# A third buffer for raw weights in a hybrid decoder block, paid with one tile of another pool

## The chip, the cores and the metric

The kernel runs on one core of a Trainium2 chip. The metric is device time in microseconds. The kernel before takes 958.78 us, the median of three runs (956.76, 958.78, 961.67). The profile shown below comes from one further execution that took 956.58 us, of which 954.4 us lie between its first and its last instruction.

## The reference, cut to what matters

One layer for 512 tokens of width 1024, all in 32-bit floats:

```
proj = rms_norm(x) @ w_in                      # 1024 x 3096 columns
o_nsa  = nsa_attention(...)                    # 8 heads, 2 KV heads: compressed, selected, window
o_rwkv = rwkv7_time_mix(...)                   # 8 heads, a scan over 512 tokens
x = x + concat(o_nsa, o_rwkv) @ w_out          # 1024 x 1024
x = x + cross_attention(rms_norm(x), rms_norm(mem))   # w_q, w_kv, w_o; 256 memory tokens
h = rms_norm(x)
x = x + (silu(h @ w_gate) * (h @ w_up)) @ w_down      # hidden width 2816
out = rms_norm(x)
```

## The kernel before, in words

**Products in halves.** Each weight and each activation is split into two fp32r parts, a high one and a low one, and a product is three matmuls: high by high, high by low, low by high. So every weight tile passes through three steps before TensorE can use it. A DMA on SP's queue brings 512 KB of raw weights into a tile `w` of the tag `W` (`wload`, line 373). ScalarE casts it into `wh` (tag `WH`, line 339). VectorE subtracts to get `wl` (tag `WL`, line 340). After the subtraction the raw tile is free and the next load into it may start. There are two buffers of each of the three tags.

**The order of the dense products** is the string `ORDER` and the list `items` behind it: the input projection (`L`, `C`, `r`, `m`, `K`, `q`, `v`), the keys and values of the memory (`X0` to `X7`, then `V00` to `V03` and `V10` to `V13`), the output projection of the mixers (`o00` to `o07` for the first 256 tokens, `o10` to `o17` for the rest), then the query and output projections of the cross attention, and the FFN. The generator `bulk` (line 399) walks through this list. Before the products of item n it emits the split of item n+1 and the load of item n+2:

```
            if ld:
                halves(n + 1)
                yield from load(n + 2)
                yield from run(W[n])
                n += 1
```

An item of `w_out` or of the value part of `w_kv_x` is 12 matmuls of 512 columns, an item of the input projection or the FFN 24.

**Who goes first.** `bulk` is one of several generators. Others are `start` (first norm), `rwkv_pair`, `inverse` and `chain` (the RWKV scan, 8 chunks in a row), `attention` with its 16 units (four head pairs by four query blocks), `mem_load`, `norm` and `xatt`. A small planner (`Threads.run`) chooses which generator emits next, by a number (0 for the chain, 2 for the attention, 3 for `bulk`, 4 for the memory norm) and by a clock that adds up matmul costs. The tile framework then orders each engine's instructions, sets every semaphore and gives every tile a slot.

**Tile accounting.** A generator that needs tiles yields a request such as `dict(Q=1)` and goes on only when the planner's count allows it; `th.free(Q=...)` gives back. The planner's count of `Q` starts at `NQ - 7`, as seven of the `NQ` tiles are in use from the start. A tile of tag `Q` is 4 KB per partition, and so is one of tag `W`. The lines that matter here:

```
    tQ = mk("Q", NQ)
    tW = mk("W", 2)
...
        th.free(Q=16, U=4, A=1)          # end of chain(): AR, AM and BKt of four head pairs
...
            th.free(Q=2 if jp < 3 else 6)   # unit(): after the scores of a head pair's last block
...
            yield dict(Q=1)
            oT[jp] = qpair("oT")         # unit(): output of a head pair, read out of PSUM tile pv
            split(*oT[jp], pv)
            th.done(f"o{jp}", 1.5)
```

A unit makes its scores and then waits for the event `o{jp - 1}`, since the PSUM tile `pv` is one for all head pairs. At most three units are open at a time (`KU = 3`).

Of the kernel before, what the change touches and what calls it, by code (L numbers as in the profile page):

```python
# [18 lines left out]
KD = D // 128  # L19
RW0 = 1304  # L20
CW = -0.5 * math.exp(-0.5)
NQ, NT, NU = 29, 10, 4
C_ID, C_TRI, C_BONE, C_CEN, C_MASK, C_VAL = 0, 128, 256, 384, 512, 640


# [39 lines left out]
class Threads:  # L65
# [28 lines left out]
    def run(self):  # L94
        while self.q:
            for t in self.q:
                if isinstance(t[3], str) and t[3] in self.ev:
                    t[2], t[3] = max(t[2], self.ev[t[3]]) + ADJ.get(t[5].split()[0] + ":%d" % t[6], 0.0) + ADJ.get(t[5] + "/%d" % t[6], 0.0), None
            live = [t for t in self.q if self.fits(t)]
            assert live, (self.pools, [(t[5], t[6], t[3]) for t in self.q])  # L100
            ready = [t for t in live if t[2] <= self.clock]
            if not ready:
                self.clock = min(t[2] for t in live)
                continue
            t = min(ready, key=lambda t: (t[0], t[1]))
            if self.dense(t) < DENS:
                t = max(ready, key=lambda t: (t[5] == "bulk", -t[0], -t[1]))
            if t[3]:
                for p, n in t[3].items():
                    if p in self.pools:  # L110
                        self.pools[p] -= n
                t[3] = None
            self.mark(t[5] + ":%d" % t[6])
            t[6] += 1
            self.cur = t[5]
            try:
                with self.ahead(PR.get(t[5].split()[0], 0)):
                    y = next(t[4])
            except StopIteration:
                self.q.remove(t)  # L120
                continue
            if isinstance(y, (str, dict)):
                t[3] = y
            else:
                t[2] = self.clock + y * MUL.get(t[5].split()[0], 1.0) + ADJ.get(t[5].split()[0] + ":%d" % t[6], 0.0) + ADJ.get(t[5] + "/%d" % t[6], 0.0)


def _body(ctx, tc, I, out, dbg=None, upto=99, mark=lambda s: None):
# [10 lines left out]
    def nm(s):  # L139
        cnt[0] += 1  # L140
        return f"{s}_{cnt[0]}"

    def mk(tag, bufs, pool=None):
        def f(shape=(128, 512), dt=F32, n=tag):
            return (pool or pp).tile(list(shape), dt, tag=tag, bufs=bufs, name=nm(n))
        return f
# [8 lines left out]
    tT = mk("T", NT)  # L155
    tU = mk("U", NU)
    tI = mk("WI", 1)
    tW = mk("W", 2)
    tH = mk("WH", 2, hp)
    tL = mk("WL", 2, hp)  # L160
    t5 = mk("s512", 6)
# [237 lines left out]
    def bulk(items, first):  # L399
        todo = [i for i in items if i[0]]  # L400
        raw, W = {}, {}

        def load(n):
            if n < len(todo):
                if len(todo[n]) > 2:
                    yield todo[n][2]
                raw[n] = todo[n][0]()

        def halves(n):
            if n < len(todo):  # L410
                W[n] = raw[n]()

        W[0] = first
        yield "xn0"
        yield from load(1)
        n = 0
        for ld, run, *_ in items:
            if ld:
                halves(n + 1)
                yield from load(n + 2)  # L420
                yield from run(W[n])
                n += 1
            else:
                yield from run(None)
# [1181 lines left out]
    W0.extend([(ALLP, 0, wcols("w_in", RW0 + c, 128))] for c in (1536, 1664))  # L1606
    th.add(0, "start", ordered(start()))
    th.add(3, "bulk", bulk(items, W0))
    th.add(2, "att", attention())
    th.run()  # L1610
# [28 lines left out]
```

## Time and profile before

| | us |
|---|---|
| median of three runs | 958.78 |
| the profiled execution | 956.58 |
| its span, first to last instruction | 954.4 |
| TensorE busy in the span | 908.5 |
| VectorE busy | 508.5 |
| ScalarE busy | 400.9 |
| GpSimd busy | 80.8 |

All positions below are microseconds from the start of the span. The stages on this scale: first norm and RWKV inputs to about 185, attention and scan to about 378, memory values and output projection to about 468, cross attention to about 592, FFN to the end. Matmuls overlap in the trace, so a mean duration of one is longer than the distance from one to the next; for a rate, the busy time of a stretch is divided by its count. A number in square brackets behind a row of the timeline is the engine's idle time just before it, with what ended it.

### The profile page before, as it was taken

The page shows a single profiled execution, that of the slowest core. Times are in us where ns is not written, and L with a number is a line of the kernel's source. Part 1 is how long each engine was busy: PE and PEld are TensorE (multiplying, and loading weights), DVE is VectorE, ACT ScalarE, POOL GpSimd, SP SyncE. Part 2 cuts the span into 40 slices and gives each one's busy share as a digit, 9 for nine tenths or more (in the row PEclk, how much of TensorE's full clock was granted, in tenths as well). Part 3 has the DMA queues.
Part 4 walks back from the last instruction along what each step waited for, and adds up shares of the span by engine and source line. Part 5 has one row for each costly group of instructions (what it writes and reads, how often), then busy time and mean ns, then how long its engine had stood idle before and what let it go on. Part 6 is the DMA issues. An engine that isn't in the chain of part 4 may idle for free.

```text
span 954.4 us, 14532 instructions
## 1 busy us (share of the span) xinstructions
PE 908.5 (95%) x5797; PEld 741.3 (78%) x5797; DVE 508.5 (53%) x991; ACT 400.9 (42%) x738; POOL 80.8 (8%) x128
## 2 busy tenths in 40 slices
PE   6999999999999988879899999999999999999997
PEld 4778777777778766757788888888888888888885
DVE  5366676788565776355555555443343443422235
ACT  4355444347567886334444433332323323212121
POOL 5121110000240010010200002000000000000002
PEclk9999999999999999999999999999999999999998
DMA  7222445736203121774431141323333333242332
GB/s 228 58 66 69 124 113 140 180 89 135 89 3 100 35 56 47 203 214 140 126 89 48 64 142 36 111 89 92 108 89 109 89 90 109 89 129 91 92 107 88
DMA packets 125405, 97.19 MB, mean 102 GB/s; under 512 B 23531, under 2 KB 109873, under 8 KB 125339
## 3 DMA queue, kind: packets, MB, share of 16 engines
q1 hardware_dynamic: 122714, 91.80, 33.8%
q10 hardware_dynamic: 2624, 4.48, 1.8%
q8 instruction: 45, 0.74, 0.4%
q14 instruction: 22, 0.17, 0.1%
HBM read 90.22 MB, written 4.48 MB: 99 GB/s over the span
## 4 chain that ended last, share of the span: by engine, by line
PE 80%; ACT 6%; DVE 6%; DMA 5%; issue 2%; POOL 2%; SPq 0%; ACTq 0%; POOLq 0%; DVEq 0%
PE pj L207 41%; PE acc L207 16%; PE pv L207 3%; DMA w<-in_w_out_dram 2%; ACT wh L339 2%; PE pt L211 2%; PE kx L207 2%; PE sc L207 2%; PE ps L207 2%; PE vg L207 1%; PE ch L207 1%; DVE wl L340 1%; DMA w<-in_w_kv_x_dram 1%; PE tr L211 1%; PE xs L207 1%
## 5 line engine op out<-in xcount | busy, mean ns | idle before, releaser
L207 PE MATMUL pj<-xn,wh 128*128 128x512 f32 (+1 forms) x1280 | 293.3, 378 | 0.8 <-DVE xn L340 0.5
L340 DVE TENSOR_TENSOR wl<-w,wh 128x1024 fp32r<-128x1024 f32 (+1 forms) x130 | 158.5, 1219 | 198.5 <-ACT wh L339 113.8
L207 PEld LDWEIGHTS pj<-xn,wh 128*128 128x128 f32 x1280 | 227.4, 190 | 46.3 <-issue 2.7
L339 ACT CAST wh<-w 128x1024 fp32r<-128x1024 f32 (+1 forms) x131 | 137.0, 1046 | 277.9 <-PE pj L207 144.8
L207 PE MATMUL pj<-xn,wl 128*128 128x512 f32 (+1 forms) x640 | 154.9, 379 | 0.0
L207 PEld LDWEIGHTS pj<-xn,wl 128*128 128x128 f32 x640 | 113.8, 188 | 21.8 <-issue 1.6
L207 PE MATMUL acc<-wh,hid 128*128 128x512 f32 x288 | 68.2, 389 | 0.0
L207 PEld LDWEIGHTS acc<-wh,hid 128*128 128x128 f32 x288 | 54.1, 188 | 11.2
L1474 DVE SCALAR_TENSOR_TENSOR th<-th,pj 128x512 f32<-128x512 f32 x22 | 15.1, 688 | 75.7 <-PE pj L207 75.7
L207 PE MATMUL acc<-wh,oT 128*128 128x512 f32 x128 | 34.6, 413 | 9.4 <-ACT wh L339 6.6
L207 PEld LDWEIGHTS acc<-wh,oT 128*128 128x128 f32 x128 | 24.2, 197 | 16.9 <-ACT wh L339 8.7
L1105 ACT ACTIVATE S<-S,mx 128x128 f32<-128x128 f32 (+3 forms) x64 | 35.3, 552 | 4.3 <-DVE mx L1103 4.2
L207 PE MATMUL acc<-wl,hid 128*128 128x512 f32 x144 | 35.6, 389 | 0.0
L1535 POOL TENSOR_TENSOR xr<-xr,gain 128x512 f32<-128x512 f32 x4 | 5.2, 1288 | 345.3 <-DVE ss L1532 345.3
L1103 DVE CUSTOM_DVE_ANT_0 S<-ps,Bt 128x128 f32<-128x128 f32 (+3 forms) x64 | 29.7, 483 | 8.5 <-PE ps L207 8.3
L207 PE MATMUL ps<-K,q 128*128 128x512 f32 (+2 forms) x96 | 29.7, 390 | 3.4 <-DVE mx L1103 2.3
L207 PEld LDWEIGHTS acc<-wl,hid 128*128 128x128 f32 x144 | 27.0, 188 | 5.6
L207 PE MATMUL pv<-S,Vt 128*64 128x128 f32 x320 | 30.4, 284 | 0.3 <-ACT S L1146 0.2
L211 PE MATMUL pt<-ident,S 128*128 128x128 f32 x160 | 25.8, 280 | 4.2 <-ACT S L1146 4.2
L339 ACT CAST hid<-th 128x512 fp32r<-128x512 f32 x22 | 13.7, 621 | 31.7 <-DVE th L1474 31.7
L211 PEld LDWEIGHTS pt<-ident,S 128*128 128x128 f32 x160 | 18.1, 140 | 9.4 <-ACT S L1146 5.3
L280 POOL TENSOR_TENSOR ss<-ss,kst 128x1 f32<-128x1 f32 x14 | 7.7, 551 | 208.1 <-DVE ss L279 207.1
(298 smaller groups left out, 1302.5 us busy)
## 6 DMA issues: line engine op xcount, KB each, us to landing
w<-in_w_gate_dram SPq DMA_DIRECT2D x22, 512.0 KB, 3.9
w<-in_w_up_dram SPq DMA_DIRECT2D x22, 512.0 KB
w<-in_w_down_dram SPq DMA_DIRECT2D x22, 512.0 KB, 3.5
w<-in_w_in_dram SPq DMA_DIRECT2D x18, 512.0 KB, 5.2
w<-in_w_kv_x_dram SPq DMA_DIRECT2D x16, 512.0 KB, 4.0
w<-in_w_out_dram SPq DMA_DIRECT2D x16, 256.0 KB, 5.1
w<-in_w_out_dram SPq DMA_DIRECT2D x8, 512.0 KB, 3.7
w<-in_w_q_x_dram SPq DMA_DIRECT2D x8, 512.0 KB, 3.9
```

The costliest lines, as they stand in the source:

```text
L207: return pin(PE.matmul(o, lhsT=l, rhs=r, start=start, stop=stop, skip_group_check=True), c)
L211: return pin(PE.transpose(o, i, idn), 0.109 if i.shape[0] > 64 else 0.056)
L280: G.tensor_tensor(ss[:, 1:2], ss[:, 0:1], mhalf, op=ALU.pow)
L339: seq(A, A.copy(H, src))
L340: i = (eng or V).tensor_sub(L, src, v32(H))
L1103: V.tensor_tensor_reduce(out=s, in0=p[:, br - b0], in1=Bt[:, a, n - 1::-1], scale=-1.0, scalar=3e38, op0=ALU.add, op1=ALU.min, accum_out=m ...
L1105: A.activation(s, s, AF.Exp, bias=mx[:, a, br + 1:br + 2], scale=-1.0, accum_out=sm[:, a, br + 1:br + 2])
L1474: V.scalar_tensor_tensor(t, t, 0.5, p, op0=ALU.mult, op1=ALU.mult)
L1535: G.tensor_tensor(x, x, gf[0][:, cs], op=ALU.mult)
```

## The change

The tag `W` gets three tiles in place of two, the pool `Q` 28 in place of 29 (and the planner's count starts at 21 in place of 22). `bulk` emits the load of item n+3 where it emitted that of item n+2, with one more load ahead of the loop. `WH` and `WL` keep two tiles each. Nothing else differs.

```diff
-NQ, NT, NU = 29, 10, 4
+NQ, NT, NU = 28, 10, 4
...
-    tW = mk("W", 2)
+    tW = mk("W", 3)
...
         W[0] = first
         yield "xn0"
         yield from load(1)
+        yield from load(2)
         n = 0
         for ld, run, *_ in items:
             if ld:
                 halves(n + 1)
-                yield from load(n + 2)
+                yield from load(n + 3)
                 yield from run(W[n])
                 n += 1
```

## Rows read from the trace of the kernel before

**Rows 1.** The page: the span, and TensorE's busy time, share and count.

```profile
span 954.4 us, 14532 instructions
...
PE 908.5 (95%) x5797; PEld 741.3 (78%) x5797; DVE 508.5 (53%) x991; ACT 400.9 (42%) x738; POOL 80.8 (8%) x128
```

**Rows 2.** Busy time by stretch (start:end, length, engines, clock, DMA share, GB/s).

```profile
300.00:380.00 80.00, 73.56 (x564) 58.89 (x564) 54.60 (x170) 64.89 (x154) 6.76 (x9) 1.00 0.18 50
380.00:460.00 80.00, 68.01 (x290) 52.77 (x289) 43.47 (x57) 31.27 (x45) 5.43 (x6) 0.98 0.66 181
...
592.00:828.00 236.00, 236.00 (x1070) 196.57 (x1069) 92.64 (x110) 73.54 (x89) 0.00 (x0) 1.00 0.33 96
```

**Rows 3.** Chain of waits, 378 to 462: start, length, what.

```profile
390.20 5.09 DMA w<-in_w_out_dram
...
395.40 1.06 ACT wh L339
...
396.49 1.24 DVE wl L340
```

**Rows 4.** Tile w, 378 to 462: time from issue to landing.

```profile
DMA to landing us min/median/max: 3.6/4.1/5.8
```

**Rows 5.** Waits of TensorE, 380 to 460: total us, times, longest.

```profile
PE acc L207 <- ACT wh L339: 6.6, 5, 2.6
PE acc L207 <- DVE vx L340: 2.8, 1, 2.8
```

**Rows 6.** Waits of ScalarE and of SP's queue, 380 to 460.

```profile
ACT wh L339 <- DMA w<-in_w_out_dram: 18.7, 8, 4.5
ACT wh L339 <- DMA w<-in_w_kv_x_dram: 9.3, 4, 3.4
...
SPq L373 <- DVE wl L340: 40.3, 17, 6.5
```

**Rows 7.** Busy time by stretch, finer, columns as in rows 2.

```profile
392.00:421.00 29.00, 22.92 (x96) 17.55 (x96) 13.96 (x15) 10.14 (x11) 0.00 (x0) 1.00 0.87 235
421.00:450.00 29.00, 25.68 (x111) 20.58 (x112) 16.44 (x24) 13.27 (x23) 4.08 (x4) 0.94 0.54 147
```

**Rows 8.** Busy time by stretch at the slow clock.

```profile
430.80:436.00 5.20, 5.20 (x18) 4.19 (x19) 3.08 (x4) 1.73 (x4) 0.08 (x1) 0.67 0.47 124
```

**Rows 9.** Timeline around 391, 430 and 439 us.

```profile
391.84 1.04 ACT L339 CAST wh<-w 128x1024 fp32r<-128x1024 f32 x1 [3.44 <-PE vx L207]
392.80 1.07 ACT L339 CAST vx<-vx 128x512 fp32r<-128x512 f32 x2
...
429.69 1.04 ACT L339 CAST wh<-w 128x1024 fp32r<-128x1024 f32 x1
...
430.79 3.67 PE L207 MATMUL acc<-wh,oT 128*128 128x512 f32 x8 [2.56 <-ACT wh L339]
...
438.87 1.99 PE L207 MATMUL acc<-wh,oT 128*128 128x512 f32 x8
```

**Rows 10.** Tiles oT, ch, zy: durations ns, first and last start us.

```profile
L339 ACT CAST oT<-pv x4: 577/582/587, 257.6 to 377.8; 128x512 fp32r<-128x512 f32 x4
...
L207 PE MATMUL ch<-uv,BKt x112: 219/222/271, 249.4 to 288.2; 128*64 128x64 f32 x112
...
L836 ACT COPY VT<-zy x8: 348/372/373, 250.7 to 301.2; 128x256 f32<-128x256 f32 x8
```

**Rows 11.** Busy time by stretch around the scan, columns as in rows 2.

```profile
257.60:285.00 27.40, 27.02 (x498) 21.98 (x498) 18.53 (x65) 18.35 (x51) 9.57 (x17) 1.00 0.01 3
...
301.00:340.00 39.00, 35.92 (x276) 29.39 (x274) 28.02 (x104) 33.65 (x92) 3.27 (x6) 1.00 0.14 40
```

**Rows 12.** Groups on TensorE, 257.6 to 301: busy us, mean ns, idle before.

```profile
L207 PE MATMUL ps<-K,q 128*128 128x512 f32 (+2 forms) x23 | 7.8, 408 | 0.0
L207 PE MATMUL pv<-S,Vt 128*64 128x128 f32 x64 | 5.8, 284 | 0.0
L211 PE MATMUL pt<-ident,S 128*128 128x128 f32 x33 | 5.6, 284 | 0.2 <-ACT S L1146 0.2
```

## The prediction

> **What bounds the kernel now.** I read the page first: TensorE is busy 908.5 of 954.4 us [rows 1], so a better supply of weights can win at most what TensorE now idles on weights, some of the 45.9 us that are left. Next I read the busy times by stage. In the long FFN stretch TensorE is busy 236.00 of 236.00 us [rows 2]: there the weights are never late and a third buffer is worth nothing. Between 300 and 380 it idles 6.4 us, but ScalarE is busy 64.89 of 80 there, and this is attention work. Between 380 and 460 it idles 12.0 us, the DMA engines are busy 66% of the time, and ScalarE and VectorE have room [rows 2]. This is the stage of the memory's values and of the output projection, whose items have 12 matmuls for 512 KB in place of 24.
>
> The third view was the chain of waits in that stage. It doesn't run over TensorE but in a loop, nearly without a break from 381 to 424: a load of 5.09 us, the cast of 1.06, the subtraction of 1.24, and the next load, which starts as the subtraction ends [rows 3]. SP's queue waits 40.3 us for subtractions and the casts 28.0 us for loads [rows 6]. So here the two raw buffers set the pace. The waits of TensorE show what it costs: 6.6 us in five waits for casts, and one of 2.8 us for the read-out of the values [rows 5].
>
> **The change part by part.** *The loop with three buffers.* One turn is the landing, 4.1 us in the median [rows 4], plus 1.06 and 1.24 [rows 3], with about 0.1 us between: 6.5 us. Two buffers give an item every 3.25 us, three one every 2.2. TensorE needs 22.92 / 96 x 12 = 2.87 us for an item [rows 7]. With two buffers the loop is the slower of the two by 0.4 us an item, with three it is the faster; even at the longest landing, 5.8 us, it is (5.8 + 2.4) / 3 = 2.7. So the loads stop setting the pace. Four of the five waits for casts, 6.6 - 2.56 = 4.0 us, lie where the loop runs, and I take them as gone. What is late next is TensorE itself. Bounds: 0 if the loads only queue longer (a rival below), 4.0 if all goes.
>
> *The fifth wait.* The cast at 429.69 ends a wait of 2.56 us, and the eight matmuls behind it take 3.67 us against 1.99 for eight others [rows 9]; the granted clock of that stretch is 0.67, a mix of its two levels [rows 8]. Together 2.56 + 1.7 = 4.2 us. But no DMA wait stands at that cast: it follows the norm's work in ScalarE's queue. If the raw tile is there earlier, the cast can be placed ahead of that work; if the order on ScalarE stays, nothing changes. Bounds 0 and 4.2; I take the middle, 2.1. The Trainium skill ("TensorE: Matmul & The Clock Gate", section on HAM oscillation) says that waits for DMA between short groups of matmuls send the array back to half clock, so that a stall is paid twice; the trace agrees, with 0.67 right behind the wait. By that rule the 1.7 us go with the wait or stay with it, never alone, so that term would be 0 or 4.2.
>
> *The read-out at 392.* The cast of the first `w_out` item runs at 391.84, just ahead of the casts of `vx` at 392.80 that TensorE waits for [rows 9]. With its raw tile earlier it may run sooner, and the read-out moves up by at most its own 1.04 us. Bounds 0 and 1.0; I take 0.8, as ScalarE idles 3.44 us ahead of it.
>
> *The start.* One more load is issued ahead of the loop, behind the loads of x on the same queue. TensorE isn't short of weights there, so I take 0, with 1 us either way because its bytes fall among others.
>
> *The load order on SP.* Each load waits for the same subtraction as before, only its content is one item further on. Nothing on SP's queue is held longer; cost 0.
>
> *One tile less in `Q`.* This is the part that costs. I counted the tiles from the code at the moment when the first attention output, `oT[0]`, is read out (257.6 us [rows 10]). Held are: AR 4, AM 8, BKt 4 and VT 2 for the scan, K 4, Vt 1, q of three head pairs 3, bias tiles of two head pairs 2. That is 28, and `oT[0]` is the 29th. All of `Q` is full at that point, and with 28 there is no slot. The planner's count says the same: `unit` asks for `Q=1` with the count at 1, and with one less it must wait. The next tiles to come back on the attention's side are two after the scores of unit 7, but units 4, 5 and 6 hold the three places (`KU`) and wait for `o0`: unit 7 can't begin. So the release has to come from the scan: in the planner at its end, on the chip with the last use of BKt at 288.2, or with the last copy at 301.2 [rows 10]. The first output is late by 30 to 44 us on the old clock, less as far as the scan, with TensorE more to itself, ends sooner. Behind the waiting instruction stand the products of units 4 to 6 with the values and everything of units 7 to 15.
>
> What hides it: TensorE's total work is the same, and the stretch costs only what TensorE idles. It is full now (27.02 of 27.40 us [rows 11]); the attention's largest groups in it, up to 301, are 7.8 + 5.8 + 5.6 = 19.2 us [rows 12]. These are what would fall out at the worst: +19.2. In their place can come the scores of units 5 and 6, the memory norm and the eight key items `X0` to `X7`, which wait only for that norm; they don't need `o0`. If all is filled, 0. Later the attention has more to do per microsecond on ScalarE, which is already busy 33.65 of 39 us from 301 to 340 [rows 11], so part of it comes back as waits. A gain isn't excluded, if the scan ends early. I take +4, near the filled end, since the filler is larger than the hole but starts late, behind the norm. Bounds -1 and 19.
>
> The sum: -4.0 - 2.1 - 0.8 + 4.0 = -2.9 us. The profiled execution took 956.58 us, 2.2 less than the median; it would go to 953.7. Put on the median, 958.78 - 2.9 = 955.9; I predict 956.
>
> **The rivals.** *The hole is filled.* The framework's own order brings `X` items and scores forward, the tile comes free with BKt, and nothing is lost: -6.9, and with all of the fifth wait and the read-out -9.2. That gives 950 to 952, say 951. For it: the framework orders each engine by what is ready, and TensorE idles 0.4 us in that stretch now [rows 11]. Against it: the key items can't start before the memory norm, which has the last place in the planner.
>
> *The attention decides (slower).* `oT[0]` waits for the whole scan, to 301 on the old clock; TensorE has only the scan and little else, and afterwards ScalarE, at 86% [rows 11], can't make up for it. If 14 of the 19.2 us [rows 12] come out as idle time and the gains stay as forecast, this is +7: 966. It decides against the change as soon as the idle time added between 257 and 378 passes the 6.9 us of gains. For it: the count of tiles has no slack, and offsets in the planner were set for the old order. Against it: conserved work, and eight items of filler.
>
> *The third buffer doesn't speed up the loads.* From 392 to 421 the DMA engines are busy 0.87 at 235 GB/s [rows 7]. If that is as much as these transfers give, loads issued earlier land no earlier, the 4.0 us stay, and with 4 for the tile and 2.1 for the fifth wait the time is 958.78 + 1.9, say 960.5. At full share, 29 x 0.87 = 25.2 us would do for the 29; that is 3.8 less, close to what I claim, so the margin is thin. Against it: the share is 0.54 in the next stretch [rows 7], and an earlier start spreads the bytes. The Trainium skill ("DMA: Bandwidth & Descriptors", section on bandwidth) has 341 GB/s for 1 MB transfers, above the 235 / 0.87 = 270 that the row allows; by the page the 6.8 MB of the stretch would take an estimated 20 us and this rival would fall, by the row it stays.
>
> **How the numbers follow.** Chances: forecast 0.42, hole filled 0.22, attention decides 0.24, loads no faster 0.12. The forecast's own range is 952 to 961: its gain from 1 to 7, its price from 0 to 8. What a measurement of this kernel can tell from no change is about 0.5%, 4.8 us: below 954.0 is faster, above 963.6 slower. Faster: 0.22 from the filled hole and 0.10 of the forecast, 0.32. Slower: 0.24 from the attention, and 0.04 from the ends of the two middle cases, 0.28. The rest, 0.40, is no difference. The range of 8 in 10 reaches from 948, a little below the filled hole, to 967, just past the attention's 966.
>
> **What would show it.** Right on the loads: between 380 and 460 the casts wait far less than 28.0 us for loads, the chain leaves the loop of load, cast and subtraction, and the output projection's first eight items follow each other at 2.8 to 2.9 us. Right on the tile: the first read-out `oT<-pv` moves from 257.6 to somewhere between 275 and 300, the key products start earlier than the end of the scan, and TensorE shows some microseconds of idle time between 257 and 300 that it doesn't have now. I am wrong if that read-out stays near 257 (the count is wrong), if the casts still wait as long for DMA, or if time moves in the FFN, where I expect nothing at all.

## The result, and the profile after

The changed kernel takes 964.04 us (median of 20 runs, 958.62 to 969.56), the kernel before 957.59 on the same chip (20 runs). The ratio is 1.0064, 95% interval 1.0046 to 1.0081: slower by about 6 us, where I had forecast 2.9 us faster. The profiled execution took 965.93 us.

The page after, span and TensorE's row: 9.7 us more of span, 7.2 us more busy time for the same 5797 matmuls.

```profile
span 964.1 us, 14550 instructions
...
PE 915.7 (95%) x5797; PEld 746.7 (77%) x5797; DVE 510.3 (53%) x991; ACT 402.7 (42%) x738; POOL 78.3 (8%) x128
```

Busy time by stretch, columns as in rows 2, of the kernel after:

```profile
185.00:245.00 60.00, 52.49 (x389) 43.54 (x388) 52.65 (x185) 32.47 (x95) 0.73 (x3) 0.94 0.48 107
245.00:300.00 55.00, 48.53 (x950) 39.97 (x949) 29.37 (x84) 27.16 (x70) 14.15 (x26) 0.94 0.22 67
300.00:380.00 80.00, 71.22 (x571) 56.58 (x571) 51.73 (x158) 60.65 (x134) 6.46 (x12) 0.98 0.28 83
380.00:460.00 80.00, 77.63 (x442) 61.01 (x441) 51.64 (x114) 44.14 (x96) 5.78 (x5) 0.98 0.49 145
592.00:828.00 236.00, 236.00 (x1096) 197.60 (x1095) 94.32 (x115) 73.70 (x92) 3.14 (x3) 1.00 0.31 92
```

Two of these stretches of the kernel before, which the prediction had not looked at:

```profile
185.00:245.00 60.00, 55.56 (x612) 46.87 (x612) 47.09 (x172) 31.26 (x97) 2.13 (x6) 0.97 0.50 114
245.00:300.00 55.00, 54.06 (x895) 43.70 (x896) 36.96 (x128) 35.97 (x102) 14.63 (x27) 1.00 0.19 60
```

From 380 to 460 TensorE is now busy 77.63 us against 68.01 [rows 2], but with 442 matmuls against 290, as attention work has moved into this stretch; the gain of the stage is better read from events, below. The FFN is unchanged. Time is lost ahead: between 185 and 300 TensorE idles 14.0 us where it idled 5.4, and its clock is lower.

The waits of TensorE after, 380 to 460. The five waits for casts and the one for the read-out [rows 5] are gone, and the longest wait left is this one, for a subtraction:

```profile
PE acc L207 <- DVE wl L340: 2.0, 1, 2.0
```

The tiles after, first and last start: the first attention output is read out at 312.2 instead of 257.6, beside the last copy of the scan, which moved from 301.2 to 312.6 [rows 10].

```profile
L339 ACT CAST oT<-pv x4: 569/584/592, 312.2 to 419.5; 128x512 fp32r<-128x512 f32 x4
...
L837 ACT COPY VT<-zy x8: 372/373/390, 266.4 to 312.6; 128x256 f32<-128x256 f32 x8
```

**Where the time goes.** I followed five events through both traces (first or last start, from the views by tile). `sol` is the first product of the inverse, on VectorE. `lt`, and `y` behind it, are the 32x32 matmuls that finish the inverse. `ch<-uv` is the first update of the scan's state, `zy<-AM,uv` ends the scan, and `xs<-kx` is the first score of the cross attention. The last column, from the last scan product to that score, holds the gains that the prediction summed up; the hole that the missing tile leaves lies ahead of it, in the scan. From that score to the end of the span both take 472 us.

| | inverse starts (`sol`) | `lt` first | `ch<-uv` first | last `zy<-AM,uv` | first `xs<-kx` | `lt` to `ch` | `zy` to `xs` |
|---|---|---|---|---|---|---|---|
| before | 174.5 | 224.6 | 249.4 | 299.4 | 482.1 | 24.8 | 182.7 |
| changed | 185.4 | 234.8 | 265.2 | 311.9 | 491.6 | 30.4 | 179.7 |

Behind the scan the change gains 3.0 us; up to its end it loses 12.5. Some 7 of these are there at the last score of the RWKV pairs (`sc`, 165.1 and 172.0). Most of that the runs don't tie to the change: q28, befburst and zburst below, in which TensorE has the order of the kernel before up to there, are at `sc` at 168.3 to 170.1. The nine kernels with loads three ahead from the start lie at 168.2 to 172.6, the eight others at 164.8 to 170.1. The clock is part of it (last section). The rest has two places, and the scan itself, from the first `ch<-uv` to the last `zy`, is 3.3 us shorter.

*Place one: the inverse.* Its input `nb` is loaded by SP. SP's queue before, and after:

```profile
166.59 0.80 SPq L669 DMA_DIRECT2D ndr<-AM  x2
167.48 2.43 SPq L913 DMA_DIRECT2D K<-K  x4
170.01 0.53 SPq L713 DMA_DIRECT2D nb<-ndr  x1
```

```profile
170.48 3.33 SPq L670 DMA_DIRECT2D ndr<-AM  x4
173.90 3.82 SPq L914 DMA_DIRECT2D K<-K  x4
177.77 1.16 SPq L373 DMA_DIRECT2D w<-in_w_in_dram  x2
179.03 0.43 SPq L714 DMA_DIRECT2D nb<-ndr  x1
```

One item further ahead puts the weights of the first `v` item in front of `nb`. From the last `ndr` write (166.9 and 173.4) to the inverse's first instruction it takes 7.6 us before and 12.0 after, and VectorE waits for it. The timeline of VectorE after (number in brackets: idle before; it was 0.56):

```profile
185.37 0.21 DVE L721 TENSOR_TENSOR sol<-nb,yb 128x31 f32<-128x31 f32 x1 [5.65 <-DMA nb<-ndr]
```

*Place two: `y`.* This is a step of the scan's preparation, 128 matmuls of 32x32, just behind `lt`. TensorE after stops in it, 11 matmuls before its end:

```profile
252.77 0.50 PE L207 MATMUL y<-AM,LT 32*32 32x32 f32 x19
255.54 0.53 PE L207 MATMUL y<-AM,LT 32*32 32x32 f32 x11 [2.28 <-issue]
256.00 0.69 PE L207 MATMUL ch<-zv,AM 64*64 64x64 f32 x8
```

"issue" means that no semaphore was missing. The stretches around it after (length, TensorE busy, clock, DMA share, GB/s) show DMA traffic at full share until the stop, and the lower of the two clock levels (1.2 GHz) behind it:

```profile
249.00:251.00 2.00, 2.00 (x121) 1.00 1.12 368
251.00:253.30 2.30, 2.21 (x79) 1.00 1.02 404
253.30:255.50 2.20, 0.00 (x0) 0.90 0.13 45
255.50:262.00 6.50, 6.46 (x42) 0.51 0.01 3
```

Two queues are of kind "instruction"; one of them, q8, has packets of 16 KB, 45 in the whole execution. Between 249.5 and 253 none of its packets starts; from 253 to 254.6, as the traffic ends, there is one:

```profile
q1 hardware_dynamic: 64, 0.20, 32.8%
q8 instruction: 1, 0.02, 4.3%
```

In the kernel before, a packet of q8 is the only one of any queue between 241 and 243.5, and `y` hardly stops:

```profile
PE y L207 <- issue: 0.3, 1, 0.3
```

So my reading is: TensorE's next instructions come by DMA, and here they queued behind data. No view names the engine that a packet is for, but two counts over the traces bear the reading out. TensorE runs 11594 instructions (5797 matmuls and as many weight loads), 258 for each of the 45 packets (the row is of the page after):

```profile
q8 instruction: 45, 0.74, 0.3%
```

And in all fourteen profiles in which `y` has a wait for "issue" (0.2 to 3.2 us), here and below, its matmuls go on 1.2 to 1.5 us after a packet of q8 has landed, however long the stop was: here the packet lands at 254.3, before at 243.0, and `y` goes on at 255.54 and 244.31. So, as far as times can show it, the packet is what the stop waits for. What filled the engines is again on SP's queue, before and after:

```profile
233.37 1.02 SPq L373 DMA_DIRECT2D w<-in_w_kv_x_dram  x2
237.29 0.35 SPq L1199 DMA_DIRECT2D mem<-in_norm_mem_g_dram  x1
249.90 0.37 SPq L373 DMA_DIRECT2D w<-in_w_kv_x_dram  x1
250.32 1.05 SPq L1202 DMA_DIRECT2D mem<-in_mem_dram  x2
```

```profile
242.74 2.29 SPq L373 DMA_DIRECT2D w<-in_w_kv_x_dram  x3
246.47 0.35 SPq L1200 DMA_DIRECT2D mem<-in_norm_mem_g_dram  x1
246.87 0.90 SPq L1203 DMA_DIRECT2D mem<-in_mem_dram  x2
```

Before, the third key load stood on the queue for 12 us, waiting for one of the two raw buffers, and held the two `mem` loads back: 1.5 MB ahead of `y`. With a third buffer nothing waits, and 3 MB leave in one go, beside `y`.

### The profile page after: what moved, and what is told of

It is laid out like the page before. It is cut to its first block, busy times and chain, and to the rows that moved or that the text cites. A ratio compares the mean times of both kernels' runs of the same rounds, so it can differ in the third digit from the quotient of the medians.

```text
span 964.1 us, 14550 instructions
## 1 busy us (share of the span) xinstructions
PE 915.7 (95%) x5797; PEld 746.7 (77%) x5797; DVE 510.3 (53%) x991; ACT 402.7 (42%) x738; POOL 78.3 (8%) x128
## 4 chain that ended last, share of the span: by engine, by line
PE 47%; DVE 1%; POOL 1%; issue 1%; POOLq 0%; ACT 0%; DVEq 0%
PE pj L207 30%; PE acc L207 14%; PE xs L207 1%; PE xo L207 1%; POOL xr L1536 1%; PE xpt L211 0%; PE tr L211 0%; DVE xr L1545 0%; DVE sq L1533 0%; DVE xr L1531 0%; DVE wl L340 0%; POOL ss L1539 0%; POOL xs L294 0%; POOL ss L280 0%; ACT xs L293 0%
## 5 line engine op out<-in xcount | busy, mean ns | idle before, releaser
L1104 DVE CUSTOM_DVE_ANT_0 S<-ps,Bt 128x128 f32<-128x128 f32 (+3 forms) x64 | 29.7, 483 | 6.2 <-PE ps L207 5.8
L207 PEld LDWEIGHTS pv<-S,Vt 128*64 128x64 f32 x320 | 20.3, 140 | 14.1 <-ACT S L1147 5.2
L339 ACT CAST hid<-th 128x512 fp32r<-128x512 f32 x22 | 13.7, 621 | 31.7 <-DVE th L1475 31.7
```

Source lines behind the costliest of these rows:

```text
L207: return pin(PE.matmul(o, lhsT=l, rhs=r, start=start, stop=stop, skip_group_check=True), c)
L339: seq(A, A.copy(H, src))
L1104: V.tensor_tensor_reduce(out=s, in0=p[:, br - b0], in1=Bt[:, a, n - 1::-1], scale=-1.0, scalar=3e38, op0=ALU.add, op1=ALU.min, accum_out=m ...
```

## The experiments

Each kernel was timed in turn with the kernel before on one chip; a ratio stands with its interval. Half-clock time is 2 x (1 - mean granted clock) x span, the time spent at the lower level if the rest is at the upper one. The kernel before, timed beside each group, has a median of 19.1 us of it beside q28 to w3n2, 26.8 beside v0late to early3, 24.9 beside aftblk to aftboth and 22.9 beside zburst to zn2blk.

### One part of the change at a time

**q28**, the kernel before with one `Q` tile less:

```diff
-NQ, NT, NU = 29, 10, 4
+NQ, NT, NU = 28, 10, 4
```

> The kernel before with 28 tiles of Q in place of 29, two raw buffers, loads two items ahead. Theory A (the missing tile costs): the first read-out of pv moves from 257.6 us to the end of the scan, as in the changed kernel (312.2), TensorE idles some 5 us more between 245 and 300, and with none of the 4 to 6 us won in the output projection the time is 8 to 13 us above before. Theory B (the earlier loads disturb the order of the first 245 us, the tile costs little): within 3 us of before, since no load moves here; vg starts near 182 as in before.

Measured: 955.48 us, 0.9985 (0.9963 to 1.0007). The first read-out moved to 303.1, as counted, and it costs nothing that can be measured here.

**w3q29**, the changed kernel with the tile given back (it still fits):

```diff
-NQ, NT, NU = 28, 10, 4
+NQ, NT, NU = 29, 10, 4
```

> The changed kernel with 29 tiles of Q (the 4 KB fit beside the third raw buffer). Theory A: the first read-out of pv is back near 258 to 268, the gain of the output projection stays, and the time is 3 to 7 us below before. Theory B: the scan's input from DRAM (nb) still stands behind one more weight load on SP's queue, vg still starts 6 to 8 us late, and the time is 0 to 5 us above before.

Measured: 962.71 us, 1.0067 (1.0045 to 1.0089). The whole loss is there without the tile.

**w3bkt**, the changed kernel with the scan's BKt given back to the planner earlier:

```diff
+            if c == 6:
+                th.free(Q=4)
...
-        th.free(Q=16, U=4, A=1)
+        th.free(Q=12, U=4, A=1)
```

> The changed kernel (28 tiles) in which the scan gives the four BKt tiles back in the planner after their last use (chunk 6) and not at its end. Theory A: the first read-out of pv comes 10 to 15 us earlier than in the changed kernel (near 300), and the time falls by 1 to 4 us against it. Theory B: same time as the changed kernel, within 2 us, because what is lost is lost before 245.

Measured: 959.32 us, 1.0038 (1.0015 to 1.0061), the first read-out at 302.8. It says little: the interval touches that of the changed kernel.

**w3n2**, three buffers and 29 tiles, loads still two items ahead:

```diff
-                yield from load(n + 3)
+                yield from load(n + 2)
```

> Three raw buffers, 29 tiles of Q, but each load emitted two items ahead as before. The third buffer then only frees a load from waiting for a subtraction. Theory A: half of the gain, 1 to 4 us below before, as the position of the load in SP's queue is the old one. Theory B: as its order is the old one in the first 245 us, this one is the better of the two kernels with 29 tiles, 2 to 6 us below before.

Measured: 954.09 us, 0.9968 (0.9944 to 0.9991). So the buffer itself helps; the 1% between this kernel and w3q29 comes from emitting the loads one item earlier. But w3n2 has the stop at `y` too, 2.45 us, so the third buffer alone is enough for it. It also follows that the stop isn't what sets these two kernels apart: w3q29 has one of 1.72. What sets them apart in the traces is the inverse's later start (last `ndr` to `sol` 7.8 us and 11.4) and the clock (30.5 us of half-clock time against 41.3); how much of the 1% belongs to each isn't shown.

### Where loads three ahead hurt

**v0late**: as w3q29, but the load of the first `v` item is emitted one item later, so that `nb` stands ahead of it again.

```diff
-                yield from load(n + 3)
+                for m in () if n == 23 else (26, 27) if n == 24 else (n + 3,):
+                    yield from load(m)
```

> Three W buffers, 29 Q tiles, loads three items ahead as in the kernel with ratio 1.0067, but the load of v0's weights alone is emitted one item later, so that on SP's queue nb <- ndr (the inverse's input) stands ahead of it again, as in the kernel before; the order of everything ahead of that point stays. Theory SP (one weight load ahead of nb on SP's queue starts the inverse late): from the first ndr issue to the inverse's first sol 14.3 -> about 10.4 us, the scan's first ch<-uv about 4 us earlier (264 -> 260), ratio 1.0067 -> 1.0025. Theory order (the loss is spread over the order of casts and head's work on DVE and ACT from the start on): the 14.3 may fall, but the ratio stays 1.005 to 1.007. Theory late (the loss arises behind 300 us): 1.006.

**nbpool**: as w3q29, with `nb` on another queue.

```diff
-        now(nc.sync.dma_start(nb, ndr))
+        now(G.dma_start(nb, ndr))
```

> Same kernel with loads three items ahead, 29 Q tiles, but nb <- ndr is issued from POOL's queue and so stands behind no weight load at all. Theory SP: as the kernel with v0's load later, 14.3 -> about 10.4 us and ratio 1.0025; a ratio below that if the cmp and K DMAs on SP also gain from it. Theory order: 1.005 to 1.007. If POOL's wait for ndr holds up POOL's own work (memsets of yb and pc), up to 2 us of it comes back.

Measured: 956.84 us, 0.9987 (0.9956 to 1.0018), and 961.16 us, 1.0009 (0.9981 to 1.0037), against 1.0067 for w3q29. Both undo the inverse's delay (last `ndr` to first `sol` 8.3 and 7.3 us, 11.4 in w3q29) and both win 0.6 to 0.8% by their medians. That is more than the 4 us that the queue explains. But the scan's first `ch<-uv` didn't move (265.2 and 265.1 against 264.1), since both still stop at `y` (2.3 and 3.2 us). The delay of place one is there, and the two kernels without it are clearly faster than w3q29; but their traces don't show that the inverse's start is the cause, nor its size.

**late3** and **early3**: three ahead only from the X items on, and only up to the `v` items.

```diff
-                yield from load(n + 3)
+                for m in (n + 2,) if n < 30 else (32, 33) if n == 30 else (n + 3,):     # late3
+                for m in (n + 3,) if n < 30 else () if n == 30 else (n + 2,):           # early3
+                    yield from load(m)
```

> Three W buffers, 29 Q tiles; loads two items ahead up to q1's, three ahead from the X items on (the part in which the prediction saw the gain). Theory early (the loss of three ahead arises in the first 265 us): no loss, ratio 0.995 to 0.998, like three buffers with loads two ahead (0.9968) or a little better; 380 to 460 us keeps PE at 75 to 78 us. Theory late (three ahead disturbs X, V and output projection): 1.003 to 1.006.

> The reverse: three items ahead up to the v items, two ahead from q1's on; three W buffers, 29 Q tiles. Theory early: keeps the whole loss, 1.005 to 1.008. Theory late: 0.996 to 0.999.

Measured: late3 943.94 us, 0.9842 (0.9803 to 0.9881), far better than any theory said. early3 953.12 us, 0.9945 (0.9915 to 0.9975): it was to keep the whole loss and kept none, although its `nb` stands behind the `v` load (last `ndr` to first `sol` 11.5 us). So the theory of the inverse alone fell here. What late3 and early3 share, and w3n2 and w3q29 lack, is that `y` doesn't stop (0.3 us in both): in late3 a fourth key load blocks SP's queue ahead of `mem`, in early3 there are two key loads in place of three.

### The burst beside `y`, taken away and added

**aftblk**: the changed kernel with a single swap on SP's queue, the fourth key load ahead of the `mem` loads. The order of TensorE's work is the same, instruction by instruction.

```diff
-                yield from load(n + 3)
+                for m in (34, 35) if n == 31 else (n + 4,) if n in (32, 33) else () if n == 34 else (n + 3,):
+                    yield from load(m)
```

> The changed kernel as it is (28 Q tiles, three W buffers, three items ahead), with one difference: the fourth of the w_kv_x loads that follow the inverse stands ahead of the two mem loads on SP's queue instead of behind them; it waits there for a buffer, so that the 1 MB of mem starts about 12 us later. The order of PE's work is the same. Theory burst (3 MB in one go around 245 to 253 us make PE's own instructions late: y <- issue 2.3 us in the changed kernel, 0.3 before, and half clock behind it): y <- issue falls to 0.3, no half clock at 255 us, half-clock time of the runs from about 38 to 25 us, ratio 1.0064 -> 1.000 to 1.002. Theory queue (the loss is the inverse that starts 4 us late): 1.005 to 1.007 stays.

Measured: 958.69 us, 0.9999 (0.9977 to 1.0021) against 1.0064. SP's queue, and TensorE at `y` and behind it:

```profile
236.30 3.06 SPq L373 DMA_DIRECT2D w<-in_w_kv_x_dram  x3
241.84 0.35 SPq L1201 DMA_DIRECT2D mem<-in_norm_mem_g_dram  x1
253.67 0.37 SPq L373 DMA_DIRECT2D w<-in_w_kv_x_dram  x1
254.09 1.05 SPq L1204 DMA_DIRECT2D mem<-in_mem_dram  x2
```

```profile
245.50:249.00 3.50, 3.44 (x156) 1.00 0.02 6
249.00:257.00 8.00, 8.00 (x92) 1.00 0.27 77
```

No stop, no half clock in this stretch, and `lt` to `ch<-uv` is 25.2 us where it was 30.4. The inverse still starts late (10.9 us from the last `ndr` to `sol`). The half-clock time of all runs fell less than expected, to a median of 30.6 us from 37.6.

**befburst** was to add the burst to the kernel before, with three copies of 512 KB that nothing reads, behind the gain load:

```diff
+        for i in range(3):
+            d = dp.tile([128, 1024], F32, name=f"dum{i}")
+            after(nc.sync.dma_start(d, I["w_down"][0, i * 128:i * 128 + 128, :]), dep)
```

> The kernel before, with three copies of 512 KB from w_down to scratch memory in DRAM added on SP's queue right behind the gain load of mem, which nothing reads: 1.5 MB more at 238 to 245 us, as much as the third buffer lets through there. Theory burst: y <- issue rises from 0.3 to 1.5 to 3 us, 7 to 17 us of half clock follow it, ratio 1.004 to 1.008. Theory queue: the copies lie beside other work, 0.999 to 1.001.

**aftX3** and **aftboth** emit the third key load later, and aftboth the first `v` load too:

```diff
-                yield from load(n + 3)
+                for m in () if n == 32 else (35, 36) if n == 33 else (n + 3,):                            # aftX3
+                for m in () if n in (23, 32) else (n + 2, n + 3) if n in (24, 33) else (n + 3,):          # aftboth
+                    yield from load(m)
```

> The changed kernel with one w_kv_x load (the third of those behind the inverse) emitted one item later, so that it stands behind the mem loads: 2.5 MB instead of 3 MB before y. Theory burst: y <- issue at most 0.5 us (as in the kernel with three ahead up to the v items only, 2.5 MB and 0.3 us), ratio 0.996 to 1.002. Theory queue: 1.005 to 1.007.

> As the last one, and v0's weights load one item later as well, so that nb <- ndr stands ahead of it. If burst and queue are two losses that add: 2 to 4 us below the last one, ratio 0.992 to 0.999; if the burst was all of it: the same ratio as the last one.

Measured: befburst 960.96 us, 1.0012 (0.9988 to 1.0037); aftX3 962.74, 1.0051 (1.0023 to 1.0079); aftboth 961.51, 1.0025 (1.0002 to 1.0048). All three missed what they were built for. In befburst the copies went out at 255.5, behind the key load that waits for a buffer: after `y`, which stopped 0.3 us as ever. In aftX3 and aftboth the `mem` loads went out at 244.4 and 243.4, with `y` from 247.6 and 244.1, so the traffic still ran beside it, and it stopped 2.4 and 2.8 us. It isn't the sum of bytes that counts, then, but whether the engines are full while `y` runs. aftboth lies 2.5 us below aftX3 by the ratios and 1.2 by the medians, with intervals that overlap: the best that I have on the size of place one. befburst, with 1.5 MB of copies that don't fall beside `y`, costs nothing that is clear of the noise.

**zburst** adds it in the right place: the kernel before, same instructions on TensorE in the same order, one copy of 2 MB right behind the first two key loads.

```diff
+        d = dp.tile([512, 1024], F32, name="dum")
+        after(nc.sync.dma_start(d, I["w_down"][0, 0:512, :]), dep)
         after(nc.sync.dma_start(gm, bcast(I["norm_mem_g"], 1024)), dep)
```

> The kernel before, with one copy of 2 MB from w_down to scratch memory in DRAM (read by nothing) on SP's queue right behind the two w_kv_x loads at 234 us; PE's instructions and their order are those of the kernel before. Theory burst: the DMA engines are then still full at y's start (240.9 us) and for 2 to 4 us more, y <- issue rises from 0.3 to 1.5 to 3 us, 7 to 17 us of half clock follow, and the ratio is 1.003 to 1.008. If a burst alone is harmless: 0.999 to 1.002.

Measured: 963.22 us, 1.0059 (1.0039 to 1.0079): the loss of the changed kernel, in the kernel before. The stop and the clock, in its timeline and its stretches:

```profile
246.85 0.47 PE L207 MATMUL y<-AM,LT 32*32 32x32 f32 x17
249.24 0.38 PE L207 MATMUL y<-AM,LT 32*32 32x32 f32 x13 [1.92 <-issue]
```

```profile
239.00:246.00 7.00, 6.94 (x187) 1.00 1.18 419
246.00:248.50 2.50, 1.32 (x53) 1.00 0.03 7
248.50:250.00 1.50, 0.76 (x17) 0.96 0.00 0
250.00:262.00 12.00, 12.00 (x78) 0.50 0.32 92
```

Over the profiles of all kernels here, `lt` to `ch<-uv` falls in two groups: 24.6 to 26.6 us in the eight where `y` stops at most 0.3 us (before, q28, late3, early3, aftblk, befburst, zlate28, zn2blk), 29.7 to 36.4 in the nine where it stops 1.7 or more (changed, w3n2, w3q29, w3bkt, v0late, nbpool, aftX3, aftboth, zburst).

### The change with its first part left as before

**zlate28**: the sizes of the change (28 tiles, three buffers), loads three ahead only from the X items on, as in late3.

```diff
-        yield from load(2)
...
-                yield from load(n + 3)
+                for m in (n + 2,) if n < 30 else (32, 33) if n == 30 else (n + 3,):
+                    yield from load(m)
```

> The changed kernel (28 Q tiles, three W buffers) with loads two items ahead up to q1's and three ahead from the X items on; in it the fourth w_kv_x load waits ahead of the mem loads as in the kernel before. Theory burst and queue: no y <- issue above 0.5, half-clock time of the runs 12 to 25 us, ratio 0.982 to 0.992. If the tile matters once the rest is gone: 0.995 or more.

**zn2blk**: as w3n2, but three ahead for the X items, so that the fourth key load blocks the queue.

```diff
-                yield from load(n + 2)
+                for m in (33, 34) if n == 31 else (35,) if n == 32 else (36,) if n == 33 else () if n == 34 else (n + 2,):
+                    yield from load(m)
```

> Three W buffers, 29 Q tiles, two items ahead (ratio 0.9968), with three ahead for the X items alone, so that the fourth w_kv_x load waits ahead of the mem loads. Theory burst: y <- issue 2.5 -> 0.3, half-clock time 30 -> 15 to 22 us, ratio 0.983 to 0.992, so most of the way to the kernel with three ahead from the X items on (0.9842). If that one gained by the loads further on: 0.994 to 0.998.

Measured: zlate28 954.45 us, 0.9951 (0.9934 to 0.9969); zn2blk 949.19 us, 0.9908 (0.9887 to 0.9929). Neither stops at `y`. zn2blk came out as the theory of the burst had it. zlate28 gains less than expected (and has 28.6 us of half-clock time, not 12 to 25), which is the outcome that its last sentence gave to the tile. late3 differs from it by the tile alone, though it was timed on another chip: TensorE's waits from 300 to 460 in zlate28

```profile
PE pv L207 <- ACT S L1147: 3.9, 4, 1.2
PE acc L207 <- DVE wl L340: 3.1, 2, 2.0
PE pt L211 <- ACT S L1147: 2.7, 1, 2.7
```

stand against 1.2 us for `pt<-S`, 2.0 for `acc<-wl` and none for `pv<-S` in late3, where the first read-out is at 254.6 in place of 299.3.

| | tiles, buffers | `lt` to `ch` | last `zy` | `zy` to `xs` | ratio |
|---|---|---|---|---|---|
| before | 29, 2 | 24.8 | 299.4 | 182.7 | 1 |
| q28 | 28, 2 | 26.6 | 302.8 | 181.0 | 0.9985 |
| w3q29 | 29, 3 | 33.4 | 312.7 | 175.5 | 1.0067 |
| w3n2 | 29, 3 | 30.7 | 305.3 | 174.0 | 0.9968 |
| late3 | 29, 3 | 24.8 | 296.3 | 173.9 | 0.9842 |
| changed | 28, 3 | 30.4 | 311.9 | 179.7 | 1.0064 |
| aftblk | 28, 3 | 25.2 | 302.1 | 181.3 | 0.9999 |
| zlate28 | 28, 3 | 26.6 | 299.0 | 181.1 | 0.9951 |

## Why the prediction was wrong

**The step that failed** is "The load order on SP": "Each load waits for the same subtraction as before, only its content is one item further on. Nothing on SP's queue is held longer; cost 0." It looked at the waiting weight loads alone. What its terms left out stands behind and between them. Held longer: `nb`, behind a `v` load that had stood behind it. Held less long: the `mem` loads, which one blocked load had kept away from `y` by chance. The second is worth as much as the whole net loss: taking the burst away brings 1.0064 to 0.9999, adding it to the kernel before brings 1.0059. It isn't the only loss, since the gains behind the scan are used up too: w3n2 stops at `y` and is still faster than before, and the loss comes when its loads are emitted one item earlier (w3q29). The step was to follow every load that is issued earlier to what it meets in the DMA engines, and the trace of before had the row for it: `PE y <- issue`, 0.3 us.

**The loop, the fifth wait, the read-out (-6.9)** were right in place and about right in size. Behind the scan, `zy` to `xs` is 182.7 us before and 173.9 to 177.9 in the seven profiles with three buffers and 29 tiles (median 175.3): 7.4 us less than before; the other two profiles with two buffers and 29 tiles, befburst and zburst, have 181.7 and 180.7, so it is 6.4 by the medians. The wait for the read-out is gone, and so are the casts' waits for loads, 28.0 us [rows 6], of which the view shows none after. The order of the output projection is another than I drew: attention work is now mixed in until 420, and only then do four items follow every 2.72 us, near the 2.87 forecast for TensorE alone. The fifth wait changed its name only: `acc<-wl` waits 1.98 us for the subtraction at 438, and from 440 to 444 the granted clock is 0.65. The Trainium skill has it that waits for DMA between groups of matmuls send the array back to half clock ("TensorE: Matmul & The Clock Gate", section on HAM oscillation). The rows at `y` agree: 6.5 us at 0.51 follow a stop of 2.3.

**The tile (+4)**: the count was right, the first read-out moved from 257.6 to 312.2, later than the 275 to 300 I gave since the scan itself ends later. The price is not one number. In the six profiles with three buffers and 28 tiles `zy` to `xs` is 178.8 to 181.3 (median 179.8), 4.5 us above those with 29, close to my +4; with two buffers the same tile is free (q28). The hole itself is in the scan, before and after:

```profile
249.40:299.40 50.00, 49.06 (x856) 1.00 0.21 66
265.20:311.90 46.70, 42.10 (x815) 1.00 0.19 56
```

TensorE idles 4.6 us there in place of 0.9 (2.4 to 4.6 in the seven profiles with 28 tiles, at most 1.5 in the ten with 29), but with 41 matmuls fewer in between the scan ends 3.3 us sooner. That where loads pace the stage anyway the hole costs nothing, and where they don't the attention's later start is what TensorE waits for, is my reading of these numbers. The part behind the scan went from 182.7 to 179.7, 3.0 us for the 2.9 of my sum, but that match is luck: it leaves out the scan, and from the first `ch<-uv` to the first `xs` it is 232.7 to 226.4, 6.3 us. With the first part left as before, zlate28 gains 0.0049 x 957 = 4.7 us.

**The rivals.** "The hole is filled" fits q28, which loses nothing by the tile, but the way it gave is not what happened: TensorE idles 4 us in the scan of q28 too, and in the changed kernel the key products start at 293.2, late in the scan. "The attention decides" named the right sign and nearly the right time (966), by the wrong cause: q28 has the late read-out without a loss. "The third buffer doesn't speed up the loads" is out. The one that came true was on no list.

**Left open.** The size of the inverse's late start: 2.5 us by aftboth and aftX3, 5 to 8 by nbpool and v0late, none to be seen in early3, nor in aftblk, which both keep it. That the 16 KB packet carries TensorE's instructions is inferred from its count and from its time beside each stop; the view doesn't name an engine. Why `sc` ends some 2 us later by the medians with loads three ahead (169.8 against 167.8) stays open too. And why late3 (0.9842) is better than its parts add up to: much of it is clock, with a median of 12.2 us of half-clock time against 26.8 of the kernel before beside it.

## What to carry to other kernels

Before a load is moved ahead, walk down its queue and write next to each entry what it was waiting for: a blocked load also spaces out what stands behind it, and a buffer more takes that spacing away. Mark in the trace where an engine runs many short instructions, since by the rows at `y` its own instructions need the DMA engines as well there, and keep bursts off that place: here that was worth some 6 us; a short wait put down to "issue" right beside full DMA traffic is the sign. Test each size by itself and together with the others: the tile cost nothing that can be measured in two surroundings (q28 against before, changed against w3q29) and some 1% in a third (zlate28 against late3).

## What the runs showed of the hardware

A stop of 2 us in which no semaphore is missing costs more than itself: `lt` to `ch` is 24.6 to 26.6 us without one and 29.7 to 36.4 with one. The same kind of wait doesn't always bring the clock down: TensorE waits 1.5 us for `thw` at 70 in the kernel before and 1.6 in the changed one, and the next ten microseconds ran at the upper level in the one profile and mostly at the lower in the other. It isn't the change: w3n2, whose TensorE has the order of the kernel before there, shows 0.66 in them, late3 with the same order 1.00. Before, then after:

```profile
70.00:80.00 10.00, 9.86 (x98) 1.00 0.33 87
```

```profile
70.00:80.00 10.00, 9.77 (x75) 0.54 0.33 86
```

The clock also explains most of the spread between runs of one kernel, for this kernel some 1%. A least-squares line through all runs of the experiments and the 20 of the changed kernel, with one level per kernel (the kernel before once for each group) and one common slope, gives 0.37 us of time per us of half-clock time and leaves 1.1 us of scatter, where the runs of one kernel scatter by 2.8. At 20 us of half-clock time each, its levels are 955.9 to 956.8 for the kernel before, 956.7 for the changed one and 946.8 for late3: by this line the changed kernel would be no slower at an equal clock, and most of its loss is in its 37.6 us of half-clock time (median of the 20). The stop at `y` accounts for part of them only. In the profiles 6.8 us of half-clock time lie between `lt` and `ch<-uv` in the changed kernel and none in the kernel before, but 17.1 and 3.4 between 30 us and `lt`; befburst, with the order of the kernel before up to there, has 13.7 in that part. So how much of the half-clock time the change brings isn't shown.
